# A decoder block's feed-forward start: a second plain pair in the first network, no queued steps behind a unit's last product, and convolution steps handed out earlier

## The chip, the cores and the metric

The kernel runs on one core of one Trainium2 chip. The metric is the device time of one execution in microseconds, the median of several runs. The kernel before takes 1319.47 us (three runs, 1318.66 to 1320.85). The profiled execution took 1317.04 us; its span, from the first to the last instruction, is 1315.2 us.

## The reference

One trunk layer on x of 512 tokens by 1024 channels, all in float32:

```
h = x + 1/2 * SwiGLU_1(rmsnorm(x))            # gate, up: 1024 -> 2816; down: 2816 -> 1024
u = rmsnorm(h)
z = u @ W_in  -> conv GLU (2 x 1024) | q | k | v | merge gates (2 x 1024)
yA = Linear(swish(LayerNorm(causal depthwise conv, 31 taps (GLU))))
yB = Linear(dilated causal window attention, 4 head slots x 3 groups)
h = h + W_o( sigmoid(gA) * yA + sigmoid(gB) * yB )
h = h + 1/2 * SwiGLU_2(rmsnorm(h))
h = h + sigmoid(rmsnorm(h) @ W_pg) * (p @ W_pp)
y = rmsnorm(h)
```

## The kernel before

**Arithmetic.** Every matrix product is float32 made of three passes on TensorE: each operand is split into a high and a low part, and high x high, low x high and high x low are added up in PSUM (`mm3`, L457/458/459, in the 512-wide form). A weight's high part `wh` is an ACT copy, its low part `wl` is either a DVE subtraction (L400 and L401) or is made by a DMA that accumulates: ACT writes the negated copy (L370), GpSimd issues a DMA that adds the weight on top (L372), ACT copies the high part (L384). `by_dma` says which weights go the second way.

**The two networks** run through `ffn(n, ...)`. Gate and up are worked out in 11 pairs of column blocks, each 1024 x 256 of both matrices. A pair comes in one of two forms.

- A *plain* pair (`plain`, called once per half): 96 matmuls of 128x512 on the normal product. It needs the two parts `xsh`, `xsl` of the input and nothing else; the row norm is multiplied onto the result later by `gated` (L815, L816, L818), which frees the pair's PSUM banks.
- A *unit* (`gate_up`): a Strassen-Winograd scheme with seven products B11, B21, T2, T1, T3, B22, T4, 24 matmuls of 128x256 each (`quarters_of`, L732, L733, L735), 168 in all. Products T2 and T1, and T3 and T4, take differences of the input's quarters. `forms` makes them: DVE subtracts (L840), ACT copies the high part `bh` (L827), DVE takes the low part `bl` (L830). The first call makes T1/T2; the function that it returns (`others`) makes T3/T4. The weights' combinations are sums and differences on DVE (`sum_one`, L338, L342, L346, L351). What a product leaves in PSUM is copied by ACT (L931) or added by DVE (L944).

The down products (`down`, L742, L743, L747, added to h by L756/L758) take five of the six rounds of hidden channels in the same seven-product form, with combinations of the hidden activations that `form_pair` makes on DVE and ACT (L663, L675, L678). One round, of the plain pair 0, is plain (`down_plain`, L993 to L1000); its operands `hidh`, `hidl` are made by `keep` (L786, L788).

**What sets the order.** `EARLY` is the number of plain pairs; `PLAN` is the order of units (`gu`) and down products (`dn`, `dp`). Side work waits in two queues of small steps. `jobs` holds `forms` and `gated`; `work(t)` gives out as many of its steps as fit into t us of a product on ACT and DVE. `later` holds `form_pair` and `keep`; `QUOTA` is how many of its steps are issued after each product of a unit. Each step is an instruction in its engine's own program, so what stands before it on that engine also delays it. In front of a product that lacks an operand, the loop `while any(q not in z for z in xn)` issues the queue at once.

**Start of network 1.** Plain pair 0 runs first. In its second half `row_block` transposes x back to rows, eight pieces: TensorE transposes into PSUM (L1096), ACT squares and sums (`Rows.add`, L628) and copies to h (L1098). The row norm's root is `token` (DVE, L632 to L604 and L871), its spread over the partitions `on_all` (two matmuls L609, L610 and an ACT copy L616) gives R. The first unit runs next, and its hooks place `token` behind B11 and, behind B21, R, `gated` and `others`, all drained at once.

**Between the networks.** The convolution is a list `bg` of 240 multiply-adds (L1141) on DVE, with a copy and a running sum for each channel block (`csum`, L1159), given out by `background(n)` beside the products of q, k, v and the merge gates. `N_QK` is how many go beside each q or k unit. Only when `bg` is empty do the gate units give out the LayerNorm's steps `lns`, at most two each: centre (L1497), square, root, L1502, Silu (L1506) and the split `cvh`, `cvl` (L474, L475). What is left of them is issued in a row ahead of the convolution's projection (`py`).

**Network 2** has its `token` and R inside plain pair 0; `gated` and `others` are queued behind it, and `work(10.9)` issues them in one block.

Of the kernel before, what the change touches and what calls it, by code (L numbers as in the profile page):

```python
# [67 lines left out]
EARLY = 1  # L68
# [4 lines left out]
PLAN = (("gu", 1), ("gu", 2), ("gu", 3), ("dn", 1), ("gu", 4), ("gu", 5), ("dn", 2), ("gu", 6), ("gu", 7), ("dn", 3),  # L73
# [6 lines left out]
QUOTA = {"T4": 2, "B11": 3, "B21": 2, "T2": 1, "T1": 3, "T3": 3, "B22": 3}  # L80
# [8 lines left out]
N_QK = ((2, 0, 1),) * 6  # L89
# [29 lines left out]
def ffn_order(n):  # L119
    out = [("gq", n, j, q) for j in range(EARLY) for q in range(4)]  # L120
    for step in PLAN:
        if step[0] == "dp":
            out += [("dp", n, step[1], x_) for x_ in range(2)]
        else:
            out += [(n, step, q) for q in PRODUCTS]
    return out
# [24 lines left out]
def block_kernel(ctx: ExitStack, tc: tile.TileContext, a, out):  # L151
# [101 lines left out]
    def by_dma(key):  # L253
        return (product(key) in BY_DMA or key[0] in POOLED + RAISED or key[:2] == ("gq", "2")
                or key[0] in ("1", "2") and key[1] == ("gu", EARLY))

# [518 lines left out]
    def ffn(n, xs, u, norm, out_, soon_=None, last_=None):  # L775
# [4 lines left out]
        def keep(j, ts, tile_=None):  # L780
            if j >= EARLY:
# [17 lines left out]
        def plain(us_, beside):  # L799

            ps = bank("pg"), bank("pu")
            for k in range(KD):
# [4 lines left out]
                for g, p in ((0, ps[0]), (4, ps[1])):  # L807
                    c = slice((g + k % 4) * P, (g + k % 4 + 1) * P)
                    mm3(p, h[:, c], l[:, c], xs[k][0], xs[k][1], k == 0, k == KD - 1)
            return ps  # L810
# [63 lines left out]
        done = []  # L874
        for half in range(2):
            us_ = [lambda i=i: slab(("gq", n, 0, 2 * half + i)) for i in range(2)]
            fs = {}
            if n == "1" and half:
                fs = {k: turns.pop(0) for k in range(KD)}
            elif n == "2":  # L880
                fs = {k: f for (at, k), f in zip(N_NORM, (token, lambda: R.append(norm.on_all()))) if at == half}
                if half == 0:
                    fs[2] = soon_
            done.append(plain(us_, fs))
            if half == (n == "1"):
                others = forms()
            if n == "2":
                work(10.9)
        hooks = {}
        if n == "1":  # L890
            while jobs:
                next_job()

            def spread(done=done, others=others):
                R.append(norm.on_all("cv"))
                gated(*done)
                while jobs:
                    next_job()
                others()
                done.clear()  # L900
            hooks = {"B11": token, "B21": spread}
        else:
            gated(*done)
# [886 lines left out]
```

## Time and profile before

| what | us |
|---|---|
| median of the runs | 1319.47 |
| the profiled execution | 1317.04 |
| its span | 1315.2 |
| TensorE matmul busy | 1273.8 (97%) |
| VectorE busy | 1054.0 (80%) |
| ScalarE busy | 765.8 (58%) |
| mean granted TensorE clock | 0.989 |

PE is TensorE, PEld its weight loads, DVE VectorE, ACT ScalarE, POOL GpSimd. A row of the timeline has the start in us, the duration, engine, line, operation and out<-in; in brackets stands how long the engine had been idle before, and which instruction ended that. In the waits of an engine stand the waiting instruction, the one that was waited for, the total, how many times, and the longest. PEclk is the granted share of the TensorE clock, 1.00 being full. A matmul's own duration overlaps its neighbours': the pace of TensorE is read from starts.

### The profile page before, as it was taken

What the parts mean: (1) busy time and instruction counts of PE and PEld (TensorE: products, weight loads), DVE (VectorE), ACT (ScalarE), POOL (GpSimd) and SP (SyncE); (2) the same over time, 40 slices, a digit from 0 to 9 for tenths busy, and PEclk for the clock granted to TensorE, in tenths of its full rate; (3) what the DMA queues carried; (4) which work ended last, traced back from release to release, by engine and by line L of the source; (5) the groups of instructions that cost most, each with busy time, mean ns of one, the idle gap of its engine ahead of it and who ended that gap; (6) DMA issues with size and microseconds to landing.
All of it is one profiled execution on the core that took longest, in us unless ns stands there. A gap on an engine that the chain in (4) does not pass through costs nothing. (4 is left out here: it accounts for less than half of the span.)

```text
span 1315.2 us, 20075 instructions
## 1 busy us (share of the span) xinstructions
PE 1273.8 (97%) x7538; PEld 1127.4 (86%) x7538; DVE 1054.0 (80%) x1714; ACT 765.8 (58%) x1116; POOL 238.9 (18%) x308
## 2 busy tenths in 40 slices
PE   8799999999999999999999998999899999999997
PEld 7698989898788889898898886878898989989786
DVE  6579898898779987878886857697689888887975
ACT  8666657566453245646465435365776766665573
POOL 0101111111122232323332221113211111111000
PEclk9899999999999999999999999999999999999999
DMA  7767776866798888988887785659878687776631
GB/s 231 170 164 179 193 192 151 218 156 169 189 208 190 197 174 192 161 175 161 179 166 173 180 202 144 161 134 219 197 188 207 148 207 171 190 200 163 158 96 64
DMA packets 122567, 230.71 MB, mean 175 GB/s; under 512 B 19304, under 2 KB 63720, under 8 KB 122472
## 3 DMA queue, kind: packets, MB, share of 16 engines
q0 software_dynamic: 47872, 144.72, 54.0%
q1 hardware_dynamic: 74312, 84.46, 20.6%
q8 instruction: 59, 0.97, 0.3%
q14 instruction: 36, 0.29, 0.1%
q10 hardware_dynamic: 288, 0.26, 0.1%
HBM read 166.46 MB, written 2.13 MB: 128 GB/s over the span
## 5 line engine op out<-in xcount | busy, mean ns | idle before, releaser
L372 POOL DMA_DIRECT2D wl<-wr x106 | 91.0, 859 | 616.0 <-ACT wl L370 460.2
L1141 DVE SCALAR_TENSOR_TENSOR acc<-glu,taps,acc 128x511 f32<-128x511 f32 (+14 forms) x240 | 161.0, 732 | 0.0
L401 DVE TENSOR_TENSOR wl<-s,wh 128x1024 fp32r<-128x1024 f32 x90 | 109.8, 1220 | 55.0 <-ACT wh L400 55.0
L732 PE MATMUL pa<-bh,wh 128*128 128x256 f32 x480 | 121.3, 289 | 10.5 <-ACT bh L827 6.0
L370 ACT ACTIVATE wl<-wr 128x1024 fp32r<-128x1024 f32 x106 | 111.1, 1048 | 22.9 <-DMA wr<-in_w_ffn_gate 11.2
L733 PE MATMUL pa<-bl,wh 128*128 128x256 f32 x480 | 121.4, 289 | 0.8 <-DVE bl L830 0.7
L370 ACT ACTIVATE wl<-wh 128x1024 fp32r<-128x1024 f32 x80 | 83.7, 1051 | 57.6 <-DMA wh<-in_w_in 29.5
L400 ACT ACTIVATE wh<-s 128x1024 fp32r<-128x1024 f32 x90 | 94.1, 1049 | 35.8 <-DMA wl<-wr 13.1
L384 ACT ACTIVATE wh<-wr 128x1024 fp32r<-128x1024 f32 x106 | 110.8, 1046 | 3.5 <-PE pd L747 1.9
L732 PEld LDWEIGHTS pa<-bh,wh 128*128 128x128 f32 x480 | 94.5, 197 | 11.2 <-ACT bh L827 6.2
L733 PEld LDWEIGHTS pa<-bl,wh 128*128 128x128 f32 x480 | 94.5, 197 | 1.4 <-DVE bl L830 1.3
L372 POOL DMA_DIRECT2D wl<-in_w_in x56 | 48.7, 870 | 222.8 <-ACT wl L370 211.3
L457 PE MATMUL pq<-xsh,wh 128*128 128x512 f32 x224 | 88.7, 396 | 0.0
L458 PE MATMUL pq<-xsl,wh 128*128 128x512 f32 x224 | 87.3, 390 | 0.0
L459 PE MATMUL pq<-xsh,wl 128*128 128x512 f32 x224 | 87.3, 390 | 0.0
L735 PE MATMUL pa<-bh,wl 128*128 128x256 f32 x480 | 69.2, 288 | 0.0
L457 PE MATMUL pg<-xsh,wh 128*128 128x512 f32 x160 | 64.2, 401 | 0.3 <-DVE xsh L485 0.3
L735 PEld LDWEIGHTS pa<-bh,wl 128*128 128x128 f32 x480 | 63.9, 198 | 0.0
L458 PE MATMUL pg<-xsl,wh 128*128 128x512 f32 x160 | 62.9, 393 | 0.8 <-DVE xsl L486 0.6
L459 PE MATMUL pg<-xsh,wl 128*128 128x512 f32 x160 | 62.5, 391 | 0.0
L742 PE MATMUL pa<-wh,bh 128*128 128x512 f32 x136 | 54.6, 401 | 8.1 <-DVE gx L758 8.1
L758 DVE SCALAR_TENSOR_TENSOR gx<-pa,half,gx 128x512 f32<-128x512 f32 x80 | 56.1, 743 | 1.8 <-PE pa L747 1.7
(360 smaller groups left out, 3813.4 us busy)
## 6 DMA issues: line engine op xcount, KB each, us to landing
wl<-wr POOLq DMA_DIRECT2D x106, 512.0 KB, 5.3
wh<-in_w_in POOLq DMA_DIRECT2D x56, 512.0 KB, 7.3
wl<-in_w_in POOLq DMA_DIRECT2D x56, 512.0 KB, 6.1
wr<-in_w_ffn_down SPq DMA_DIRECT2D x44, 512.0 KB, 5.2
wr<-in_w_ffn_up SPq DMA_DIRECT2D x84, 256.0 KB, 4.5
wr<-in_w_ffn_gate SPq DMA_DIRECT2D x82, 256.0 KB, 5.2
wh<-in_w_v POOLq DMA_DIRECT2D x16, 256.0 KB, 7.2
wl<-in_w_v POOLq DMA_DIRECT2D x16, 256.0 KB, 5.8
```

The lines of the kernel that those rows point to most:

```text
L370: A.activation(l.bitcast(F32R), h, AF.Copy, scale=-1.0)
L372: G.dma_start(to, src, accum_op=OP.add)
L384: A.activation(h, r, AF.Copy)
L400: A.activation(h, r, AF.Copy)
L401: V.tensor_sub(l, r, h.bitcast(F32))
L457: PE.matmul(ps, wh, xh, start=start, stop=False, skip_group_check=part)
L458: PE.matmul(ps, wh, xl, start=False, stop=False, skip_group_check=part)
L459: PE.matmul(ps, wl, xh, start=False, stop=stop, skip_group_check=part)
L732: PE.matmul(o, h[:, c], th, start=q in ("B11", "B21", "T1") and i == 0, stop=False, skip_group_check=True)
L733: PE.matmul(o, h[:, c], tl, start=False, stop=False, skip_group_check=True)
L735: PE.matmul(o, l[:, c], th, start=False, stop=i >= len(at) - 2, skip_group_check=True)
L1141: bg.append(lambda acc=acc, g=g, w=w, s=s: V.scalar_tensor_tensor(acc[:, s:], g[:, :S - s], w, acc[:, s:], op0=OP.mult, op1=OP.add))
```

## The change

- `EARLY` becomes 2 for network 1 and stays 1 for network 2, so network 1's pair 1 is plain and its first unit is pair 2. `PLAN` starts at unit 2, with unit 1 ahead of it for network 2 alone. Pair 1's hidden tiles go to `form` like a unit's.
- `QUOTA` gives out nothing behind T4 (before 2), and 4 behind B11 (before 3).
- The first units no longer make all seven of their low parts by accumulating DMA; only B11, B21 and T4 do, as in other units.
- Network 1: `token` stands at the start of pair 1 and R behind its k = 3; behind pair 1's first half `gated` of pair 0 is issued, and `others` is queued into the second half (`plain` now calls `work(1.36)` behind each k). The hooks in the unit are gone.
- Network 2: `gated` is queued behind the plain pair, `others` behind it, and `work(2.9)` instead of `work(10.9)` follows, so that the T3/T4 differences come out with the products of unit 1.
- `row_block` copies from PSUM with DVE, and ACT squares from h.
- Convolution: `background` gives 14 instead of 10 at c == 0, 3 instead of 2 beside the first two of six q/k places in a slot, and four more ahead of each slot's `v0` unit and of the first gate unit.

Line numbers of the changed kernel are one lower than before's up to about L870, five to nine higher behind it.

```diff
--- before.py
+++ after.py
@@ -65,19 +65,19 @@
 A11, A12, A21, A22 = range(4)
 PRODUCTS = ("B11", "B21", "T2", "T1", "T3", "B22", "T4")
 MIXED = ("B11", "T1", "T2", "B22", "T3", "B21", "T4")
-EARLY = 1
+EARLY = {"1": 2, "2": 1}
 
 
 ROUNDS = ((0, 1), (1, 2), (3, 2), (5, 2), (7, 2), (9, 2))
 
-PLAN = (("gu", 1), ("gu", 2), ("gu", 3), ("dn", 1), ("gu", 4), ("gu", 5), ("dn", 2), ("gu", 6), ("gu", 7), ("dn", 3),
+PLAN = (("gu", 2), ("gu", 3), ("dn", 1), ("gu", 4), ("gu", 5), ("dn", 2), ("gu", 6), ("gu", 7), ("dn", 3),
         ("gu", 8), ("gu", 9), ("dn", 4), ("gu", 10), ("dp", 0), ("dn", 5))
 HELD = (3, 5, 7)
 BY_ = False
 N_FORM = 10
 N_LAST = 3
 AFTER_M = {"B11": 2, "T1": 2, "T2": 2, "B22": 2, "T3": 2, "B21": 2, "T4": 2}
-QUOTA = {"T4": 2, "B11": 3, "B21": 2, "T2": 1, "T1": 3, "T3": 3, "B22": 3}
+QUOTA = {"B11": 4, "B21": 2, "T2": 1, "T1": 3, "T3": 3, "B22": 3}
 POOL_MIX = False
 POOL_SUMS = False
 
@@ -86,7 +86,7 @@
 BY_DMA = ("B11", "B21", "T4")
 
 N_GLU = (0, 0) + (6,) * 14
-N_QK = ((2, 0, 1),) * 6
+N_QK = ((3, 0, 1),) * 2 + ((2, 0, 1),) * 4
 N_V0, N_V = 4, 1
 N_TURN = 6
 N_SOON = 2
@@ -117,8 +117,8 @@
 
 
 def ffn_order(n):
-    out = [("gq", n, j, q) for j in range(EARLY) for q in range(4)]
-    for step in PLAN:
+    out = [("gq", n, j, q) for j in range(EARLY[n]) for q in range(4)]
+    for step in (("gu", 1),) * (EARLY[n] == 1) + PLAN:
         if step[0] == "dp":
             out += [("dp", n, step[1], x_) for x_ in range(2)]
         else:
@@ -251,8 +251,7 @@
         return max(c.stop for _, c, _ in srcs)
 
     def by_dma(key):
-        return (product(key) in BY_DMA or key[0] in POOLED + RAISED or key[:2] == ("gq", "2")
-                or key[0] in ("1", "2") and key[1] == ("gu", EARLY))
+        return (product(key) in BY_DMA or key[0] in POOLED + RAISED or key[:2] == ("gq", "2"))
 
     def product(key):
         return key[2] if key[0] in ("1", "2", "m") else None
@@ -778,7 +777,7 @@
         xn = [{} for _ in range(4)]
 
         def keep(j, ts, tile_=None):
-            if j >= EARLY:
+            if j:
                 waiting.append((j, ts, tile_))
                 return
             hl = [(T("hidh", F32R), T("hidl", F32R)) for _ in ts]
@@ -807,6 +806,7 @@
                 for g, p in ((0, ps[0]), (4, ps[1])):
                     c = slice((g + k % 4) * P, (g + k % 4 + 1) * P)
                     mm3(p, h[:, c], l[:, c], xs[k][0], xs[k][1], k == 0, k == KD - 1)
+                work(1.36)
             return ps
 
         def gated(pgs, pus):
@@ -871,39 +871,46 @@
             V.tensor_scalar(t, y, 0.5, None, op0=OP.mult)
             half_r.append(t)
 
-        done = []
-        for half in range(2):
-            us_ = [lambda i=i: slab(("gq", n, 0, 2 * half + i)) for i in range(2)]
-            fs = {}
-            if n == "1" and half:
-                fs = {k: turns.pop(0) for k in range(KD)}
-            elif n == "2":
-                fs = {k: f for (at, k), f in zip(N_NORM, (token, lambda: R.append(norm.on_all()))) if at == half}
-                if half == 0:
-                    fs[2] = soon_
-            done.append(plain(us_, fs))
-            if half == (n == "1"):
-                others = forms()
-            if n == "2":
-                work(10.9)
-        hooks = {}
+        def factor():
+            R.append(norm.on_all("cv" if n == "1" else "ps"))
+
+        for j in range(EARLY[n]):
+            done = []
+            for half in range(2):
+                us_ = [lambda i=i: slab(("gq", n, j, 2 * half + i)) for i in range(2)]
+                fs = {}
+                if n == "2":
+                    fs = {k: f for (at, k), f in zip(N_NORM, (token, factor)) if at == half}
+                    if half == 0:
+                        fs[2] = soon_
+                elif (j, half) == (0, 1):
+                    others = forms()
+                    fs = {k: turns.pop(0) for k in range(KD)}
+                elif (j, half) == (1, 0):
+                    fs = {0: token, 4: factor}
+                done.append(plain(us_, fs))
+                if (j, half) == (1, 0):
+                    rest = jobs[:]
+                    jobs.clear()
+                    gated(*before)
+                    while jobs:
+                        next_job()
+                    jobs.extend(rest)
+                    before = None
+                    others()
+                if n == "2" and half == 0:
+                    others = forms()
+            before = done
+        rest = jobs[:]
+        jobs.clear()
+        gated(*before)
         if n == "1":
-            while jobs:
-                next_job()
-
-            def spread(done=done, others=others):
-                R.append(norm.on_all("cv"))
-                gated(*done)
-                while jobs:
-                    next_job()
-                others()
-                done.clear()
-            hooks = {"B11": token, "B21": spread}
+            jobs.extend(rest)
+            job(lambda: (keep(1, early[1], early[1]), form()))
         else:
-            gated(*done)
             others()
-            work(10.9)
-        done = others = None
+        work(2.9)
+        done = others = before = None
 
         def both_halves(half):
             return bass.AP(tensor=R[0].tensor, offset=R[0].offset + half.start, ap=[R[0].ap[0], [0, 2], [1, 256]])
@@ -924,8 +931,6 @@
                 while any(q not in z for z in xn):
                     next_job()
                 quarters_of(p, q, wh, wl, [z[q] for z in xn])
-                if q in hooks:
-                    hooks.pop(q)()
                 if q in ("B11", "T2", "T1"):
                     t[q] = T("p")
                     A.activation(t[q], p, AF.Copy)
@@ -1004,7 +1009,7 @@
                     work(2 * k_ * 0.68)
             hid.clear()
 
-        for key in PLAN:
+        for key in (("gu", 1),) * (EARLY[n] == 1) + PLAN:
             if key[0] == "gu":
                 if key[1] == KF // 2 - 2:
                     keep(0, early[0])
@@ -1094,8 +1099,9 @@
         p = bank("tp", "cv")
         for i in range(KD // 2):
             PE.transpose(p[:, i * P:(i + 1) * P], by_class(x[4 * j + i])[:, b], ident)
-        norm.add(b, j, p)
-        A.activation(h[b][:, j * S:(j + 1) * S], p, AF.Copy)
+        V.tensor_copy(h[b][:, j * S:(j + 1) * S], p)
+        norm.add(b, j)
+        spend(0.69, 0.74)
 
     def over(xs, v, ks, us_=None):
 
@@ -1195,7 +1201,7 @@
             unit(z[2], ("win", c), us)
             glu(*z, (1,))
         if c == 0:
-            background(10)
+            background(14)
             rc, rs = tabs["cos"], tabs["sin"]
             for t in (rc, rs):
                 bg.append(lambda t=t: V.tensor_mul(t, t, R[0]))
@@ -1430,6 +1436,7 @@
         q, k = [], []
         now = Attention(q, k)
         p = bank("pq")
+        background(N_V0)
         unit(p, ("v0", s), us, beside=before.last() if before else {})
         v0 = T("v0")
         V.tensor_mul(blocks(v0), by_block(p), by_block(R))
@@ -1543,6 +1550,8 @@
     for base in (48, 40):
         for m in range(KD):
             p = bank("pg")
+            if not n:
+                background(N_V0)
             unit(p, ("win", base + m), us, beside={4: half} if n else before.last())
             t = T("sg")
             V.tensor_mul(t, p, R)
```

DVE at the start of network 1, before: the norm's R exists, and `gated` (tg, tu), the weight sums of the next unit (s) and the T3/T4 differences (t_560 on, with bl) follow.

```order
L818 TENSOR_TENSOR tu_552<-pg_272,tg_550 128x512
L818 TENSOR_TENSOR tu_553<-pu_273,tg_551 128x512
L944 TENSOR_TENSOR p_505<-p_505,pe_520 128x512
L338 TENSOR_TENSOR s_135_599<-wr_440,wr_443 128x1024
L342 TENSOR_TENSOR s_140_633<-s_135_599,wr_446 128x1024
L840 TENSOR_TENSOR t_560<-u_170,u_134 128x256
L840 TENSOR_TENSOR t_560<-u_170,t_399 128x256
L840 TENSOR_TENSOR t_563<-u_185,u_144 128x256
L840 TENSOR_TENSOR t_563<-u_185,t_400 128x256
L840 TENSOR_TENSOR t_566<-u_191,u_154 128x256
L840 TENSOR_TENSOR t_566<-u_191,t_401 128x256
L830 TENSOR_TENSOR bl_562<-t_560,bh_561 128x512
```

The same place of DVE in the changed kernel. Here pg_203 and pu_204 are the banks of plain pair 0's first half, pg_278 and pu_279 those of its second; there are six such banks, and pair 1's first half takes the other two.

```order
L421 TENSOR_TENSOR wl_495<-wr_239,wh_494 128x1024
L337 TENSOR_TENSOR s_107_498<-wr_292,wr_295 128x1024
L815 TENSOR_TENSOR tg_529<-pg_203,R_492 128x512
L815 TENSOR_TENSOR tg_530<-pu_204,R_492 128x512
L818 TENSOR_TENSOR tu_531<-pg_278,tg_529 128x512
L818 TENSOR_TENSOR tu_532<-pu_279,tg_530 128x512
L341 TENSOR_TENSOR s_128_553<-s_107_498,wr_298 128x1024
L840 TENSOR_TENSOR t_539<-u_170,u_134 128x256
L840 TENSOR_TENSOR t_539<-u_170,t_266 128x256
L840 TENSOR_TENSOR t_542<-u_180,u_144 128x256
L345 TENSOR_TENSOR wr_292<-wr_298,wr_292 128x1024
L840 TENSOR_TENSOR t_542<-u_180,t_267 128x256
```

The differences stand behind one weight sum more (s_107 ahead of tg, s_128 behind tu), and all of it is now beside a plain pair.

DVE at the merge gates and the convolution's projection, before; `sg<-pg` is a gate unit (the last of them is row sg_7770, 34 rows above this piece), `sg<-sg,pb` the attention's projection, and cv the channel blocks of the convolution.

```order
L1571 TENSOR_TENSOR sg_7310<-sg_7310,pb_7920 128x512
L1571 TENSOR_TENSOR sg_7353<-sg_7353,pb_7939 128x512
L1571 TENSOR_TENSOR sg_7407<-sg_7407,pb_7953 128x512
L1502 TENSOR_TENSOR cv_4728<-cv_4728,R_7967 128x512
L1502 TENSOR_TENSOR cv_4775<-cv_4775,R_7967 128x512
L1502 TENSOR_TENSOR cv_5920<-cv_5920,R_7967 128x512
L1502 TENSOR_TENSOR cv_5922<-cv_5922,R_7967 128x512
L1502 TENSOR_TENSOR cv_7105<-cv_7105,R_7967 128x512
L1502 TENSOR_TENSOR cv_7140<-cv_7140,R_7967 128x512
L475 TENSOR_TENSOR cvl_7978<-cv_4728,cvh_7977 128x512
L475 TENSOR_TENSOR cvl_7983<-cv_4775,cvh_7982 128x512
```

The same steps in the changed kernel, where sg_7761 is the last of the 16 gate units.

```order
L1557 TENSOR_TENSOR sg_7631<-pg_7563,R_4052 128x512
L1557 TENSOR_TENSOR sg_7664<-pg_7634,R_4052 128x512
L1509 TENSOR_TENSOR cv_4588<-cv_4588,R_7667 128x512
L1509 TENSOR_TENSOR cv_4597<-cv_4597,R_7667 128x512
L1509 TENSOR_TENSOR cv_5569<-cv_5569,R_7667 128x512
L1509 TENSOR_TENSOR cv_5576<-cv_5576,R_7667 128x512
L1557 TENSOR_TENSOR sg_7704<-pg_7670,R_4052 128x512
L1509 TENSOR_TENSOR cv_6524<-cv_6524,R_7667 128x512
L1509 TENSOR_TENSOR cv_6572<-cv_6572,R_7667 128x512
L474 TENSOR_TENSOR cvl_7711<-cv_4588,cvh_7710 128x512
L474 TENSOR_TENSOR cvl_7716<-cv_4597,cvh_7715 128x512
```

The steps from R on have moved from behind the attention's projection to among the last three gate units. The last pair of channel sums (csum) has moved from behind the 13th gate unit to behind the seventh.

DVE in network 2's first unit, before: the differences of T3/T4 stand in one block, behind `gated` (tu).

```order
L818 TENSOR_TENSOR tu_8974<-pg_8904,tg_8972 128x512
L818 TENSOR_TENSOR tu_8975<-pu_8905,tg_8973 128x512
L840 TENSOR_TENSOR t_8976<-u_8759,u_8686 128x256
L840 TENSOR_TENSOR t_8976<-u_8759,t_8876 128x256
L840 TENSOR_TENSOR t_8979<-u_8770,u_8697 128x256
L840 TENSOR_TENSOR t_8979<-u_8770,t_8877 128x256
L840 TENSOR_TENSOR t_8982<-u_8781,u_8714 128x256
L840 TENSOR_TENSOR t_8982<-u_8781,t_8878 128x256
L830 TENSOR_TENSOR bl_8978<-t_8976,bh_8977 128x512
L840 TENSOR_TENSOR t_8985<-u_8792,u_8725 128x256
L840 TENSOR_TENSOR t_8985<-u_8792,t_8879 128x256
```

In the changed kernel they stand among the unit's weight splits (wl) and weight sums (s):

```order
L840 TENSOR_TENSOR t_8869<-u_8657,t_8774 128x256
L400 TENSOR_TENSOR wl_8971<-wr_8537,wh_8970 128x1024
L840 TENSOR_TENSOR t_8872<-u_8668,u_8595 128x256
L840 TENSOR_TENSOR t_8872<-u_8668,t_8775 128x256
L400 TENSOR_TENSOR wl_9004<-s_1434_8892,wh_9003 128x1024
L337 TENSOR_TENSOR s_1451_9007<-wr_8894,wr_8897 128x1024
L840 TENSOR_TENSOR t_8875<-u_8679,u_8612 128x256
L341 TENSOR_TENSOR s_1456_9043<-s_1451_9007,wr_8900 128x1024
L840 TENSOR_TENSOR t_8875<-u_8679,t_8776 128x256
L830 TENSOR_TENSOR bl_8871<-t_8869,bh_8870 128x512
L840 TENSOR_TENSOR t_8878<-u_8690,u_8623 128x256
L840 TENSOR_TENSOR t_8878<-u_8690,t_8777 128x256
```

The first bl now stands behind wl_9004, the low part of B22's weight, and the sums s_9007 and s_9043 of the next unit.

## The prediction

> **What bounds the kernel now.** I read the page first, for the busy shares:
>
> ```profile
> PE 1273.8 (97%) x7538; PEld 1127.4 (86%) x7538; DVE 1054.0 (80%) x1714; ACT 765.8 (58%) x1116; POOL 238.9 (18%) x308
> ```
>
> TensorE is busy 97% of the span, 1273.8 us, so the most that reordering can win without touching its work is the other 3%, some 40 us, and what the granted clock costs. The waits of PE say who owns that idle time (columns: total us, times, longest):
>
> ```profile
> PE pa L742 <- DVE gx L758: 8.1, 4, 2.1
> PE pa L732 <- ACT bh L827: 6.0, 1, 6.0
> PE pa L732 <- ACT p L931: 4.3, 1, 4.3
> PE R L609 <- DVE diag L604: 2.6, 1, 2.6
> PE py L457 <- ACT cvh L474: 2.4, 1, 2.4
> PE py L458 <- DVE cvl L475: 2.2, 4, 1.6
> PE tp L1096 <- ACT gx L1098: 1.5, 2, 0.8
> ```
>
> They are few and long, and lie in four places: the first unit of network 1 (bh, diag), the first of network 2 (p), the opening of a down product after the last gate/up (gx), and the conv projection (cvh, cvl). The windows on these places give the clock (columns: length, then busy time of PE, PEld, DVE, ACT, POOL, PEclk, DMA share, GB/s):
>
> ```profile
> 40.00:72.00 32.00, 22.36 (x140) 21.02 (x139) 19.98 (x49) 16.22 (x22) 5.03 (x6) 0.79 0.73 172
> 290.00:310.00 20.00, 18.04 (x86) 14.37 (x86) 17.39 (x22) 12.70 (x15) 3.40 (x4) 1.00 0.78 194
> 380.00:810.00 430.00, 429.57 (x2244) 368.52 (x2242) 341.37 (x652) 211.13 (x354) 119.92 (x160) 1.00 0.85 180
> 800.00:820.00 20.00, 15.83 (x63) 12.01 (x63) 14.42 (x39) 11.67 (x16) 1.44 (x3) 0.91 0.64 164
> 920.00:940.00 20.00, 15.70 (x96) 14.42 (x95) 15.74 (x28) 17.02 (x22) 4.95 (x6) 0.93 0.80 183
> 1170.00:1190.00 20.00, 18.04 (x80) 14.64 (x79) 16.65 (x21) 11.87 (x15) 2.65 (x4) 0.91 0.71 178
> ```
>
> A clock of 0.79 over 32 us is 6.7 us of work lost; 0.91 over 20 us is 1.8. So a wait is followed by a stretch of half clock that costs nearly as much again. Between 380 and 810 us PE waits for nothing (429.57 of 430) and DVE is at 79%: there nothing can be won, only lost.
>
> **First network, start.** The unit lengths come from first matmuls of neighbours in the timeline: a plain pair runs 512-wide matmuls, six of them from 924.69 to 926.05; the first unit starts at 35.90, the second at 71.86, the third at 92.02.
>
> ```profile
> 924.69 0.39 PE L457 MATMUL pg<-xsh,wh 128*128 128x512 f32 x1
> ...
> 926.05 0.28 PE L732 MATMUL pa<-xsh,wh 128*128 128x256 f32 x1
> ```
> ```profile
> 35.90 0.28 PE L732 MATMUL pa<-xsh,wh 128*128 128x256 f32 x1
> ...
> 71.86 0.28 PE L732 MATMUL pa<-xsh,wh 128*128 128x256 f32 x1
> ...
> 92.02 0.28 PE L732 MATMUL pa<-xsh,wh 128*128 128x256 f32 x1
> ```
>
> A plain pair is 96 matmuls at 1.36/6 = 0.227 us, 21.8 us; an undisturbed unit is 92.02 - 71.86 = 20.2 us; the first one takes 36.0, because its own chain cannot keep up:
>
> ```profile
> 40.77 0.16 DVE L632 SCALAR_TENSOR_TENSOR m<-rows 128x4 f32<-128x4 f32 x1
> ...
> 45.00 0.16 DVE L871 TENSOR_SCALAR half<-y 128x4 f32<-128x4 f32 x1
> ...
> 48.91 0.69 DVE L815 TENSOR_TENSOR tg<-pg,R 128x512 f32<-128x512 f32 x1 [3.75 <-ACT R L616]
> ...
> 56.31 1.22 DVE L342 TENSOR_TENSOR s<-s,wr 128x1024 f32<-128x1024 f32 x1 [3.00 <-DMA wl<-wr]
> 57.45 0.42 DVE L840 TENSOR_TENSOR t<-u,u 128x256 f32<-128x256 f32 x1
> ```
>
> The norm factor takes 45.0 - 40.8 = 4.2 us on DVE, R comes back at 48.9, and the T3/T4 differences (L840) come next on DVE behind the weight sum L342, which waits 3.00 us for a DMA until 56.3. The change puts a plain pair there, which needs neither R nor differences. The same chain then runs beside the pair: the eight PSUM copies go to DVE at 0.69 each (the L815 row, also a 128x512 read of PSUM), which takes away the transposes' wait of 1.5, so pair 0 ends at about 35.9 - 1.5 = 34.4. The norm chain starts there and ends near 38.6; R's matmuls stand behind k = 4 of pair 1, by PE's count at 34.4 + 24 x 0.227 = 39.9, so they need not wait. They are two of 512 columns, 2 x 0.227 = 0.45 us. Behind the norm chain DVE has two weight splits and L337 (1.22 each, as L342), four bl (0.69, the size of L815), two differences (0.42) and the two L815 that empty pair 0's banks: 8.6 us, so they end at 38.6 + 8.6 = 47.2, or 46.3 as a step starts some 0.08 before the last one ends (57.45 against 56.31 + 1.22). PE wants the bank at 34.4 + 0.45 + 48 x 0.227 = 45.8. I take a wait of 0.9 there, between none and 1.8. Pair 1 ends at 34.4 + 21.8 + 0.45 + 0.9 = 57.6, against 71.9 now: **-14.3**. Bounds: -15.2 if nothing waits, about -8 under the first rival. In unit 2, which is now the first to need T3, the differences are queued in pair 1's second half, some 11 us (48 x 0.227) before the unit starts and 22 before its fifth product; I see no wait.
>
> [...]
>
> **Opening of the down product after the fourth group.** T4, a unit's last product, no longer hands out two queued steps (2 of the quota; B11 takes one more). In the trace DVE waits for ACT's weight copy wh, and PE for DVE:
>
> ```profile
> 297.53 1.23 DVE L401 TENSOR_TENSOR wl<-s,wh 128x1024 fp32r<-128x1024 f32 x1 [1.96 <-ACT wh L400]
> ...
> 299.56 0.47 PE L742 MATMUL pa<-wh,bh 128*128 128x512 f32 x1 [1.96 <-DVE gx L758]
> ```
>
> The same happens at this place in network 2, where the steps ahead of wh on ACT, L675's b and (not shown) bh, can be seen waiting for the sum u:
>
> ```profile
> 1175.21 0.42 ACT L675 ACTIVATE b<-u 128x256 fp32r<-128x256 f32 x1 [3.10 <-DVE u L936]
> ...
> 1179.17 0.61 PE L742 MATMUL pa<-wh,bh 128*128 128x512 f32 x1 [1.96 <-DVE gx L758]
> ```
>
> Without these steps wh is done before DVE gets to it, and both waits of 1.96 go: -2.0 in network 1, and in network 2 -2.0 and the half clock behind it, 1.8 by the 1170 window: **-5.8**. Bounds: -3 if wh is held by the DMA instead, -6. The two other L742 waits (2.1 each, behind the plain down product) are left alone: what DVE does there has the same sum.
>
> **Conv and its norm.** 31 multiply-adds of the conv (two pairs of N_QK groups, four ahead of each slot's v0, four ahead of the first gate unit, four at c == 0) run earlier.
>
> ```profile
> L1141 DVE SCALAR_TENSOR_TENSOR acc<-glu,taps,acc 128x511 f32<-128x511 f32 (+14 forms) x240 | 161.0, 732 | 0.0
> ```
>
> At 0.73 each at most that is 23 us of DVE work taken off the far end. The last channel sums come behind the 13th of the 16 gate units now, behind the 7th in the changed order, and all eight L1502 steps stand ahead of the sum of the last gate unit, not in front of the projection. So py's waits, 2.4 + 2.2, go, and the half clock (0.91 in the 800 window, 1.8): **-6.4**; -3 if one of the waits stays with its half clock. The cost lies in cover: DVE rises from 341 to 364 of the 430 us at most, if none of these steps had been in them; PE has no wait there and I cost it at nothing, up to +5 if four slots wait 1.2 each, the length of one weight sum. Two more table loads on ACT cost nothing, since ACT is at 211 of 430.
>
> **Second network, first unit.** Only T3/T4 are moved: before, they were drained while PE waited.
>
> ```profile
> 935.64 0.57 ACT L931 ACTIVATE p<-pa 128x512 f32<-128x512 f32 x1
> ...
> 946.48 0.28 PE L732 MATMUL pd<-xsh,wh 128*128 128x256 f32 x1
> ```
>
> ACT came to p only at 935.64, PE waited 4.3, and T3 ended where the sixth product starts, at 946.5. Now p comes right behind B11, so T2 need not wait: that alone is -4.3, and -1.4 of half clock (0.93 over 20 us), together -5.7. At 20.2 / 7 = 2.9 us a product, T2 ends at 934.7 and T3 could start at 937.6. But T3 wants bl, and in the changed order DVE reaches the first bl behind the weight split of B22, which waits for ACT, and ACT stands behind T2's copy: 934.7 + 0.57 for the copy + 0.6 for a bh + about 1.1 for the weight (twice the columns) = 937.0. Then follow on DVE that split, two weight sums (1.22 each) and two differences (0.42): 4.5, so bl starts at 941.5; with four bl and two differences more, 3.6, the last one ends at 945.1. Half of T3's last quarter is left then, so it ends between 946 and 948: a new wait takes the place of the old one, **+0.7**, between -5.7 (no wait) and +3 (a half clock behind it).
>
> **Sum, on the profiled execution (1317.04 us):** -14.3 - 5.8 - 6.4 + 0.7 = **-25.8**, 1291.2. The median of the runs is 1319.47, 2.43 above that execution; so **1293.7**.
>
> **Rivals.** (1) *A weight sum holds pair 1.* L337, a sum of two weight tiles for unit 2, stands ahead of the L815 steps on DVE; if its tiles are late, as at 56.31 (3.00 us), pair 0's banks are kept, PE waits up to 5 us in the middle of pair 1 and half clock costs 1.8: the start is worth 14.3 - (5 + 1.8 - 0.9) = 8.4, and the time is 1293.7 + 5.9 = 1299.6. For: the DMA was at 0.73 over 40 to 72, and two plain pairs read weights just as fast. Against: the 7 accumulating transfers of the first unit go. (2) *The conv's gain stays out:* DVE late in the slots, or the projection waits as before: +6.4 and up to 5, 1300.1 to 1305.1. For: DVE is the busiest engine after PE. Against: it has 89 us free in those 430, and no PE wait. (3) *No new wait at T3:* DVE reaches the differences in time; 1293.7 - 6.4 = 1287.3. For: DVE was busy 15.7 of 20 us at 920 to 940 with the whole block drained at once. Against: the order puts B22's split ahead of bl. (4) *The half clocks are not of these waits.* At 299.56 a wait of 1.96 stands as at 1179.17, and only the latter has lost clock beside it (1.00 in 290 to 310, 0.91 in 1170 to 1190). If the 1.8 at 800 and the 1.8 at 1170 stay, the time is 1293.7 + 3.6 = 1297.3. [...] (5) *Slower:* the steps T4 no longer takes pile up and come due at the down products. There are ten; the gain of 5.8 there goes, and from (25.8 - 5.8) / 10 = 2.0 us each the change loses: at 4.3 us each, what the drained steps cost T2 in network 2, it is 1293.7 + 5.8 + 43 = 1342.5. For: L742 already heads the waits. Against: the quota falls only from 17 to 16 a unit.
>
> **How the numbers follow.** Forecast 0.50 (its own range 1290 to 1298: nothing waits in pair 1 and the first network gains 0.9 more with 2 to 3 less at T3, or T3 costs 2 more and the down products give 2 less); rival 1 0.17, 2 0.14, 3 0.06, 4 0.09, 5 0.04. The range 1287 to 1304 holds all these but 5, the upper end of 2, and 1 and 2 together, under 0.2 in all. A measurement of this kernel tells 0.2% (2.6 us) from no change. Every case but 5 is faster by more; what is left for no change is a sum of several mishaps: 0.94 faster, 0.02 same, 0.04 slower.
>
> **What would show it.** Right: second unit's first matmul near 57.6 with clock 1.00 in 40 to 72; no wait of PE for R or bh there; the openings after the fourth group without the 1.96; py without a wait; a wait of 4 to 5.5 us in T3 of network 2, on bl. Wrong: a wait on tg in pair 1 over 2 us, PE waits between 380 and 810, or a longer list of L742 waits.

## The result, and the profile after

The changed kernel takes 1284.38 us (four runs, 1284.28 to 1289.34) against 1319.07 of before (1318.08 to 1320.85): a ratio of 0.9745, interval 0.9719 to 0.977. The forecast was 1293.7, its range 1287.0 to 1304.0: the direction was right, the gain larger than the range allowed, 34.7 us for 25.8. The profiled execution is the longest of the four, 1289.34 (span 1287.2, mean clock 0.995); the three others took 1284.28 to 1284.48 at 0.996 and 0.997. So the trace shows 27.7 us of gain, close to the forecast only because the profiled execution is 5.0 us over its kernel's median; the rest is in executions that it does not show.

What PE waits for now:

```profile
PE pa L741 <- DVE gx L757: 4.2, 2, 2.6
PE pa L732 <- DVE bl L830: 4.0, 1, 4.0
PE warm L503 <- DVE one L497: 1.1, 1, 1.1
PE pg L456 <- DVE tg L815: 0.9, 1, 0.9
PE pb L456 <- ACT xsh L476: 0.8, 1, 0.8
```

R, bh, p, cvh, cvl and tp are gone from the list. The wait on gx (DVE adds a down product's result to h, which frees the PSUM bank that PE wants next) is down from 8.1 in four to 4.2 in two. The 0.9 on tg, in the middle of network 1's pair 1, and the 4.0 on bl, in network 2's T3, are the two new waits that were forecast. The same five stages in windows:

```profile
40.00:58.00 18.00, 17.08 (x78) 13.92 (x77) 16.17 (x28) 11.80 (x16) 1.84 (x2) 1.00 0.49 118
361.00:771.00 410.00, 410.00 (x2160) 352.67 (x2159) 341.33 (x652) 210.42 (x356) 113.93 (x152) 1.00 0.83 177
780.00:800.00 20.00, 20.00 (x90) 16.54 (x90) 7.68 (x13) 6.57 (x8) 7.07 (x10) 1.00 0.96 232
900.00:925.00 25.00, 20.99 (x150) 20.49 (x150) 17.94 (x27) 14.30 (x19) 2.57 (x3) 0.86 0.47 109
1195.00:1215.00 20.00, 17.37 (x70) 13.84 (x69) 18.11 (x26) 10.05 (x13) 0.86 (x1) 0.91 0.70 188
```

The start of network 1 has lost no clock (1.00, before 0.79). PE has no wait between 361 and 771, nor at the convolution's projection (780 to 800). Lost clock has moved to T3 (0.86 over 25 us, 3.5 us) and to the last down product of network 2 (0.91 over 20, 1.8).

Read from first matmuls in the two timelines, with the forecast's terms:

| stage | forecast | by the traces |
|---|---|---|
| start of network 1, to the start of unit 2 | -14.3 | 71.86 to 57.41: -14.4 |
| the two openings after the fourth group | -5.8 | -2.2 and -3.4: -5.5 |
| other down products, both networks | 0 | -0.7, -0.9 (the third of each); -1.5 and +1.1 from the plain product on |
| from q/k/v to network 2's first unit | -6.4 | -7.7 |
| network 2's first units, to its first down product | +0.7 | +1.7 |

What is left of 28.0 us of span lies in steps of 0.5 us or less.

T3 of network 2, DVE first and then PE:

```profile
910.40 1.23 DVE L400 TENSOR_TENSOR wl<-s,wh 128x1024 fp32r<-128x1024 f32 x1 [1.54 <-ACT wh L399]
911.55 1.22 DVE L337 TENSOR_TENSOR s<-wr,wr 128x1024 f32<-128x1024 f32 x1
...
913.02 1.22 DVE L341 TENSOR_TENSOR s<-s,wr 128x1024 f32<-128x1024 f32 x1
...
914.49 0.68 DVE L830 TENSOR_TENSOR bl<-t,bh 128x512 fp32r<-128x512 f32 x1
```
```profile
915.23 0.58 PE L732 MATMUL pa<-bl,wh 128*128 128x256 f32 x1 [3.96 <-DVE bl L830]
```

The split wl of B22 waits for ACT, two weight sums follow, and bl starts at 914.49. The whole program lies 26.6 us earlier here (899.48 for 926.05), so the forecast's 941.5 is 914.9 on this axis.

### The profile page after: what moved, and what is told of

It is laid out like the page before. It is cut to its first block, busy times and chain, and to the rows that moved or that the text cites. A ratio compares the mean times of both kernels' runs of the same rounds, so it can differ in the third digit from the quotient of the medians.

```text
span 1287.2 us, 19870 instructions
## 1 busy us (share of the span) xinstructions
PE 1265.8 (98%) x7466; PEld 1122.6 (87%) x7466; DVE 1062.2 (83%) x1724; ACT 750.6 (58%) x1093; POOL 229.5 (18%) x297
## 5 line engine op out<-in xcount | busy, mean ns | idle before, releaser
L369 ACT ACTIVATE wl<-wr 128x1024 fp32r<-128x1024 f32 x101 | 106.1, 1050 | 19.9 <-DVE wl L400 5.7
L732 PE MATMUL pa<-bl,wh 128*128 128x256 f32 x456 | 113.6, 286 | 4.0 <-DVE bl L830 4.0
L731 PE MATMUL pa<-bh,wh 128*128 128x256 f32 x456 | 113.2, 285 | 0.3 <-DVE p L949 0.3
L383 ACT ACTIVATE wh<-wr 128x1024 fp32r<-128x1024 f32 x101 | 105.8, 1047 | 8.4 <-PE pd L746 6.2
L732 PEld LDWEIGHTS pa<-bl,wh 128*128 128x128 f32 x456 | 88.6, 194 | 4.5 <-DVE bl L830 4.5
L731 PEld LDWEIGHTS pa<-bh,wh 128*128 128x128 f32 x456 | 88.5, 194 | 0.5 <-DVE p L949 0.5
L456 PE MATMUL pg<-xsh,wh 128*128 128x512 f32 x176 | 70.9, 403 | 1.1 <-DVE tg L815 0.9
L457 PE MATMUL pg<-xsl,wh 128*128 128x512 f32 x176 | 69.4, 394 | 0.7 <-DVE xsl L485 0.4
L458 PE MATMUL pg<-xsh,wl 128*128 128x512 f32 x176 | 68.7, 390 | 0.0
L936 ACT ACTIVATE p<-pa 128x512 f32<-128x512 f32 x38 | 22.7, 598 | 69.4 <-PE pa L734 69.0
```

What stands on the lines that cost most here:

```text
L369: A.activation(l.bitcast(F32R), h, AF.Copy, scale=-1.0)
L383: A.activation(h, r, AF.Copy)
L456: PE.matmul(ps, wh, xh, start=start, stop=False, skip_group_check=part)
L457: PE.matmul(ps, wh, xl, start=False, stop=False, skip_group_check=part)
L458: PE.matmul(ps, wl, xh, start=False, stop=stop, skip_group_check=part)
L731: PE.matmul(o, h[:, c], th, start=q in ("B11", "B21", "T1") and i == 0, stop=False, skip_group_check=True)
```

## The experiments

**The same kernel again, and three single edits.** They ran on one chip with 14 runs of before: median 1317.92, 1312.14 to 1323.62.

> The changed kernel itself once more. Its profiled execution took 1289.3 us, three others 1284.3 to 1284.5. Theory A (half clock by chance): the waits are the same in all executions, and the 5.1 us are the half-clock stretches behind the T3 wait of network 2 (6.83 us long, 3.4 lost) and behind the last down product's wait (3.41 long, 1.7 lost), which most executions do not get: median 1284 to 1285, and a profile of a short execution shows PE idle as before within 0.5 us and one or both stretches gone. Theory B (shorter waits): a short execution has the T3 wait under 2 us or the transfers' waits gone, with the same half clock.

1286.93 (1285.48 to 1288.31), ratio 0.9774, interval 0.9753 to 0.9795: 31.0 us of gain here. Its profiled execution took 1286.55. The wait at T3 is the same to 0.01, and so is its half clock; behind the last down product the wait was 1.5 instead of 2.6, with no clock lost:

```profile
910.00:925.00 15.00, 10.99 (x72) 10.50 (x72) 9.79 (x15) 7.27 (x10) 1.71 (x2) 0.77 0.38 71
1198.00:1210.00 12.00, 10.49 (x46) 8.21 (x45) 12.00 (x16) 7.97 (x11) 0.86 (x1) 1.00 0.67 171
```

1.1 of wait and 1.8 of clock make the 2.8 us between the two profiled executions. So neither theory holds whole: behind the down product both the wait and the half clock were shorter, and the long wait at T3 is in both executions with its half clock. No execution of 1284 was profiled; that they lack part of the half clock at T3 is only suggested, by mean clocks of 0.996 and 0.997 for 0.995.

The convolution's places alone:

```diff
-N_QK = ((2, 0, 1),) * 6
+N_QK = ((3, 0, 1),) * 2 + ((2, 0, 1),) * 4
...
-            background(10)
+            background(14)
...
+        background(N_V0)
...
+            if not n:
+                background(N_V0)
```

> The kernel before with only the convolution's steps handed out earlier. Forecast's term: -6.4 us, 1312.7. Read from the two traces between the start of the q/k/v stage and network 2 it is -7.7, 1311.4. Rival (DVE in the slots pays for it): no gain, or waits of PE between 380 and 770 us of over 3 us in all.

1309.94, ratio 0.9945 (0.9927 to 0.9964), 8.0 us by the medians. First the kernel before in the stage of the attention slots, then this kernel at the projection and in the slots:

```profile
380.00:770.00 390.00, 390.00 (x2065) 336.23 (x2064) 321.24 (x604) 196.52 (x336) 110.00 (x146) 1.00 0.84 178
```
```profile
795.00:815.00 20.00, 20.00 (x90) 16.59 (x89) 7.73 (x12) 10.28 (x13) 5.66 (x8) 1.00 0.75 182
380.00:770.00 390.00, 390.00 (x2071) 336.31 (x2070) 330.82 (x624) 200.93 (x344) 110.42 (x147) 1.00 0.84 179
```

DVE does 9.6 us more in the slots at no cost to PE, and the projection runs without a wait. The rival is out. In the timelines the gain from q/k/v to network 2 is 8.3, more than the 6.4 of waits and clock. Part of that may be that a wait costs more than its listed length: two matmuls of before, at 811.98 and 814.07, start 2.1 us apart where 0.23 is the usual pace, so 1.9 is lost at a listed wait of 1.6. What the rest is was not traced.

The quota alone:

```diff
-QUOTA = {"T4": 2, "B11": 3, "B21": 2, ...
+QUOTA = {"B11": 4, "B21": 2, ...
```

> The kernel before with only the quota changed: nothing behind T4, four behind B11. Forecast's term: -5.8 us, 1313.3, both waits of 1.96 gone. From the traces of after: -2.2 and -3.4 at the two openings and 0.4 to 0.9 at each of two or three other down products, -6 to -7.5 in all, 1311.6 to 1313. Rival (steps pile up at the down products): slower, a longer list of waits of the down products.

1306.50, ratio 0.992 (0.9901 to 0.9938): 11.4 us by the medians, twice the forecast's term.

```profile
PE py L458 <- DVE cvl L475: 1.8, 2, 1.6
PE pa L742 <- DVE gx L758: 1.7, 2, 0.9
PE pd L997 <- DMA wl<-wr: 1.6, 2, 0.9
```

Gx is down from 8.1 in four to 1.7 in two: not only the two waits of 1.96 are gone, those behind the plain down product are 0.9 each for 2.1. The steps do not pile up, so the prediction's rival 5 is out too. By the timelines the two openings gave 2.2 and 3.3, as forecast; the third down product of each network 0.7 and 0.9, and the stretch of plain and last down product 2.5 and 1.2. The forecast had put these last four at nothing.

Why the waits behind the plain product fall is to be seen on DVE 15 us and more before them, where it adds up weight tiles for the last down product. In network 1, before:

```profile
330.89 1.22 DVE L338 TENSOR_TENSOR s<-wr,wr 128x1024 f32<-128x1024 f32 x1 [1.21 <-DMA wr<-in_w_ffn_down]
...
338.71 1.23 DVE L342 TENSOR_TENSOR s<-s,wr 128x1024 f32<-128x1024 f32 x1 [5.27 <-DMA wr<-in_w_ffn_down]
```

With only the quota changed:

```profile
328.50 1.23 DVE L338 TENSOR_TENSOR s<-wr,wr 128x1024 f32<-128x1024 f32 x1 [0.37 <-DMA wr<-in_w_ffn_down]
...
330.97 1.22 DVE L342 TENSOR_TENSOR s<-s,wr 128x1024 f32<-128x1024 f32 x1
```

In network 2 these waits are 1.53 and 3.91 before, and none with the quota alone. So DVE had stood idle for a load, and all its work behind that came later.

The rest of the change alone: the changed kernel with the two diffs above undone.

> The changed kernel with the quota and the convolution's places as before: what is left is the second plain pair, the PSUM copies on DVE, fewer accumulating transfers in the first units and the spread differences in network 2. Forecast: -14.3 + 0.7 = -13.6, 1305.5; by the trace of after -14.5 + 1.7 = -12.8, 1306.3, and by the short executions 3.4 less, 1303. Rival (terms not additive): under 10 us, over 1309.

1303.09, ratio 0.9897 (0.9878 to 0.9915): 14.8 us by the medians, 13.6 by the ratio of 1317.92. The terms add within the noise: 13.6 + 7.2 + 10.5 = 31.3 by the three ratios, against 29.8 for the whole change by its own.

**The spread differences of network 2.** These four ran on another chip, before 1317.55 (11 runs, 1311.75 to 1319.14).

```diff
-        work(2.9)
+        work(10.9)
```

> The changed kernel with all of network 2's queued differences issued behind the plain pair at once, as before the change. Theory (the wait only moved): T3's wait of 3.96 on bl goes, T2's wait of about 4.3 on p comes back, with about as much half clock: within 2 us of the changed kernel, 1284 to 1288. Rival (spreading was worth the forecast's -5.7): 5 us slower, 1290 to 1292.

1279.45 (1278.21 to 1281.94), ratio 0.9716 (0.9697 to 0.9735). Neither theory said this: issued in one block (the *drained* kernel from here on), the differences cost less than spread, and the kernel beats the changed one, whose eight runs in two other sets took 1284.28 to 1289.34. The traces say the same of this stage alone: from the first matmul of network 2's first unit to that of its first down product it takes 62.4 us, in the changed kernel 68.2 and 67.6. The old wait did not come back whole:

```profile
PE pa L741 <- DVE gx L757: 2.6, 2, 1.6
PE pa L731 <- ACT p L936: 1.7, 1, 1.7
```
```profile
898.00:925.00 27.00, 25.33 (x209) 25.05 (x209) 24.17 (x35) 18.57 (x26) 2.57 (x3) 1.00 0.61 157
```

T2 waits 1.7 on p, not 4.3, without lost clock. On ACT only one weight copy stands between the last bh and p:

```profile
903.74 0.63 ACT L827 ACTIVATE bh<-t 128x512 fp32r<-128x512 f32 x1 [0.58 <-DVE t L840]
904.28 1.04 ACT L399 ACTIVATE wh<-s 128x1024 fp32r<-128x1024 f32 x1
905.23 0.58 ACT L936 ACTIVATE p<-pa 128x512 f32<-128x512 f32 x1
```

Half of the differences ahead of the unit:

```diff
-        work(2.9)
+        work(5.8)
```

> The changed kernel with 5.8 instead of 2.9 us of queued steps issued ahead of network 2's first unit, so that about half of the T3/T4 differences stand ahead of the weight splits. Theory (T3 waits for what stands ahead of bl on DVE, T2 for what stands ahead of p on ACT): T3's wait falls by 1 to 2 us and T2 does not wait over 1: 1 to 3 us below the changed kernel. Rival: T2 waits as much as T3 gains, no change.

1283.94 (1283.08 to 1287.88). The wait at T3 did not fall: 4.5 in the profiled execution, 1287.88.

```profile
911.53 1.23 DVE L400 TENSOR_TENSOR wl<-s,wh 128x1024 fp32r<-128x1024 f32 x1 [1.05 <-ACT wh L399]
912.67 1.22 DVE L337 TENSOR_TENSOR s<-wr,wr 128x1024 f32<-128x1024 f32 x1
913.92 1.22 DVE L341 TENSOR_TENSOR s<-s,wr 128x1024 f32<-128x1024 f32 x1
915.07 1.29 DVE L830 TENSOR_TENSOR bl<-t,bh 128x512 fp32r<-128x512 f32 x2
```

The last two bl still stand behind B22's split and both sums. What matters is the last bl, not how many are early. The theory was right on the cause and wrong on the remedy; the rival, that T2 takes over the wait, is not seen either.

Two plain pairs in network 2 as well:

```diff
-EARLY = {"1": 2, "2": 1}
+EARLY = {"1": 2, "2": 2}
...
```

The lines left out keep the norm's steps and the first call of `forms` in network 2's pair 0.

> The changed kernel with two plain pairs in network 2 also. The differences then run beside a plain pair: T3's wait of 3.96 and the half clock behind it (3.4) go, a plain pair costs 1.6 more than a unit: -5.8 us, about 1280 where the changed kernel takes 1286. Rival (the wait moves into the pair, as 0.9 on tg in network 1, or the queue is late for the next unit): -2 or less.

1280.17 (1279.84 to 1280.89), ratio 0.972 (0.9703 to 0.9738). Waits and clock of that stage are gone, as expected:

```profile
898.00:945.00 47.00, 47.00 (x305) 43.14 (x304) 30.11 (x44) 24.59 (x36) 6.10 (x7) 1.00 0.63 145
```

It is level with the drained kernel: a plain pair takes 1.6 us more than a unit, about the 1.7 that the drained kernel waits at T2.

T4's steps dropped, B11 left at three, in the kernel before:

```diff
-QUOTA = {"T4": 2, "B11": 3, "B21": 2, ...
+QUOTA = {"B11": 3, "B21": 2, ...
```

> The kernel before with only T4's two queued steps dropped from the quota and nothing added to B11. Theory (the steps behind T4 stand ahead of what the down product's opening needs): as the whole quota edit, 9 to 11 us below before, with both waits of 1.96 gone and the wait behind the plain down product near 0.9 in place of 2.1. Rival (the steps of B11 matter, or the queue now runs over into the down products): under 6.

1310.32, ratio 0.9948 (0.9933 to 0.9963): 7.2 us, between theory and rival. The openings are clear, but the waits behind the plain product have grown to 2.9:

```profile
PE pa L742 <- DVE gx L758: 5.9, 2, 2.9
```

So T4's part gives about 7 us (6.9 by its ratio), and B11's fourth step the rest of the quota's 10.5, some 3.7 us. The two ran on different chips and their intervals touch, but the waits on gx, 2.9 each here for 0.9 each, show the step's effect in the traces.

**What holds p, where the copies are, and a fifth step.** On a third chip, before 1318.3 (9 runs, 1313.69 to 1321.3). First the drained kernel with the accumulated low parts again:

```diff
-        return (... or key[:2] == ("gq", "2"))
+        return (... or key[:2] == ("gq", "2")
+                or key[:2] == ("2", ("gu", 1)))
```

> The kernel with network 2's differences drained at once (1279.5 us), with all seven low parts of network 2's first unit made by accumulating DMA again, as in the kernel before. Theory (ACT's two extra passes per accumulated low part stand ahead of p, more than the drained differences do): T2's wait of 1.67 grows to about 4.3, with half clock behind it, 1283 to 1286. Rival (the drained differences alone hold p): the wait stays near 1.7, 1279 to 1280.

1284.61 (1282.86 to 1285.63): 5.2 us over the drained kernel by the medians, 3.2 by the ratios on the two chips, and 4.2 in the traces of this stage (66.6 us for 62.4). The wait on p is 4.6, and ACT shows why:

```profile
902.83 0.63 ACT L828 ACTIVATE bh<-t 128x512 fp32r<-128x512 f32 x1 [0.64 <-DVE t L841]
903.37 1.04 ACT L370 ACTIVATE wl<-s 128x1024 fp32r<-128x1024 f32 x1
904.31 1.04 ACT L384 ACTIVATE wh<-s 128x1024 fp32r<-128x1024 f32 x1
905.26 1.04 ACT L370 ACTIVATE wl<-wr 128x1024 fp32r<-128x1024 f32 x1
906.21 1.04 ACT L384 ACTIVATE wh<-wr 128x1024 fp32r<-128x1024 f32 x1
907.15 0.57 ACT L937 ACTIVATE p<-pa 128x512 f32<-128x512 f32 x1
```

Four weight passes stand between the last bh and p where the drained kernel has one. They are in the kernel before too:

```profile
931.32 0.63 ACT L827 ACTIVATE bh<-t 128x512 fp32r<-128x512 f32 x1 [0.64 <-DVE t L840]
931.85 1.04 ACT L370 ACTIVATE wl<-s 128x1024 fp32r<-128x1024 f32 x1
932.80 1.04 ACT L384 ACTIVATE wh<-s 128x1024 fp32r<-128x1024 f32 x1
933.75 1.04 ACT L370 ACTIVATE wl<-wr 128x1024 fp32r<-128x1024 f32 x1
934.69 1.04 ACT L384 ACTIVATE wh<-wr 128x1024 fp32r<-128x1024 f32 x1
```

The theory holds, though an accumulated low part costs ACT one pass more than a subtracted one (L370), not two: of before's wait at T2, the larger part was the accumulated low parts, which the change takes away as well.

The changed kernel with ACT's copies again:

```diff
-        V.tensor_copy(h[b][:, j * S:(j + 1) * S], p)
-        norm.add(b, j)
+        norm.add(b, j, p)
+        A.activation(h[b][:, j * S:(j + 1) * S], p, AF.Copy)
```

> The changed kernel with the eight PSUM copies of the first plain pair on ACT again, which squares from PSUM. Forecast's working: the transposes wait 1.5 again, and pair 1 inherits it, +1.5 us. Rival (the norm chain on DVE is due earlier when DVE has no copies, and the wait of 0.9 on tg goes): +0.6 or less, no difference to be told.

1285.64 (1284.7 to 1287.44), ratio 0.9751: no difference from the changed kernel's 0.9745 and 0.9774. The transposes wait again, and the wait on tg is gone.

```profile
PE tp L1101 <- ACT gx L1103: 0.9, 1, 0.9
```

The rival holds: whichever engine copies, DVE reaches tg at the same time (45.5 us here, 45.6 in the changed kernel).

The drained kernel, and the one with two plain pairs in both networks, with a fifth step:

```diff
-QUOTA = {"B11": 4, ...
+QUOTA = {"B11": 5, ...
```

> The kernel with network 2's differences drained at once (1279.5 us), with five queued steps behind B11 instead of four. Theory (the fourth step behind B11 is what cut the wait behind the plain down product from 2.9 to 0.9 by bringing the queue forward; a fifth does the same again): these two waits, 1.0 and 1.6 there, fall by 0.5 to 1 each, 1277.5 to 1279. Rival (the fifth step stands ahead of what a product needs): waits at B21 or T2 of the units, 1280 or more.

> The kernel with two plain pairs in both networks (1280.2 us), with five queued steps behind B11. Same theory: the two waits behind the plain down products, 1.2 and 0.9 there, fall by 0.5 to 1 each, 1278.5 to 1279.5; same rival, 1281 or more.

1285.77 (1283.12 to 1286.1) and 1284.05 (1281.67 to 1285.24), by the medians 6.3 and 3.9 us worse than the kernels without the step. By the ratios on the two chips that is 4.0 and 2.0, with intervals that overlap. In the traces the stretches from the plain down products on are 5.8 and 6.4 us longer in all, part of it half clock. The theory falls, and the waits at B21 or T2 that the rival named are not there either (T2 waits 1.1 on p, in the drained kernel 1.7). The waits behind the plain product are 2.9. The drained kernel with the fifth step, its waits and its weight sum on DVE:

```profile
PE pa L741 <- DVE gx L757: 5.8, 2, 2.9
```
```profile
315.58 1.23 DVE L337 TENSOR_TENSOR s<-wr,wr 128x1024 f32<-128x1024 f32 x1 [4.16 <-DMA wr<-in_w_ffn_down]
...
320.11 1.22 DVE L341 TENSOR_TENSOR s<-s,wr 128x1024 f32<-128x1024 f32 x1 [1.98 <-DMA wr<-in_w_ffn_down]
```

The drained kernel without it:

```profile
312.91 1.22 DVE L337 TENSOR_TENSOR s<-wr,wr 128x1024 f32<-128x1024 f32 x1
...
315.37 1.22 DVE L341 TENSOR_TENSOR s<-s,wr 128x1024 f32<-128x1024 f32 x1
```

DVE waits 4.16 and 1.98 for the last down product's weights, does the sum 4.7 us later, and everything behind it slips. The loads' issue on SP goes with it: in all eight profiles with four steps behind B11 and none behind T4, the third of the six loads of this stage is issued 11.4 us after the first, in both networks; in all six with another quota, 12.7 to 13.7 us after it. The queue's own waits tell what that load waits for, in the changed kernel and in the kernel before:

```profile
SPq L268 <- DVE wl L400: 4.4, 1, 4.4
```
```profile
SPq L269 <- DMA wl<-wr: 5.9, 1, 5.9
```

In all eight it waits 4.4 us for a low part that DVE subtracts, in all six others 5.8 to 6.6 us for an accumulating transfer. So the quota changes which instruction frees the third load's buffer. Why it does was not tried and stays open, and the early issue is not the whole of it: in network 2 of the changed kernel's first profile DVE still waits 3.83 us for these weights, and PE 2.6 behind the plain product.

## Why the prediction was wrong

- **Start of network 1: right.** -14.3 forecast, -14.4 in the traces, with the forecast wait of 0.9 on tg. One part of its working was idle: the PSUM copies on DVE win nothing, since the transposes' wait and the wait on tg stand for each other. That the sum fits so closely is therefore partly luck. L337 was not late; rival 1 did not happen.
- **Openings after the fourth group: right**, -5.8 forecast and -5.5 in the traces; dropping T4's steps alone clears both.
- **The failing step: "The two other L742 waits (2.1 each, behind the plain down product) are left alone: what DVE does there has the same sum."** The sum of DVE's work is the same, but not when it can start: in before's trace DVE stands idle 5.27 us at 338.71 for the weights of the last down product, a wait that the prediction did not price, and the quota changes when those weights are loaded. With the quota alone the two waits of PE there fell from 2.1 to 0.9, worth 2.5 and 1.2 us in the timelines where the forecast had nothing. The third down products, also at nothing, gave 0.7 and 0.9; PE had no wait over 0.2 us there, and what they gained from is not shown. In all the quota was worth 10.5 us by its ratio (11.4 by the medians), with an interval of 8.2 to 13.0, not 5.8.
- **Convolution: right within the noise.** 6.4 forecast, 7.2 by the ratio (4.7 to 9.6), and 7.7 and 8.3 in the traces, so perhaps a little small: waits were priced at their listed length. PE paid nothing in the slots; rival 2 did not happen.
- **Network 2: the new wait right, the cause of the gain wrong.** The wait on bl came where it was put, 4.0 us, and +1.7 for +0.7 is inside its bounds; rival 3 did not happen. But the forecast credited T2's gain to the moved differences ("Only T3/T4 are moved"). It came mostly from the accumulated low parts: with those gone and the differences drained as before, the kernel is 1279.45. The spreading itself costs 5 to 6 us here by the traces.
- **The range** had no room left for this. By the ratios the other terms together were off by about a microsecond, the quota by 5. In the second set of runs the gain was 31.0 us, which gives 1288.5 on the forecast's basis, just inside; with the first set's 34.7 it is outside. What sets the two sets apart is not shown.
- **Rival 4**, that half clock is not of these waits, was too simple: it comes with waits, but not with each of them nor in each execution, as the last section shows. So the half clock in the forecast's terms (1.8 at the opening in network 2, 1.8 at the convolution) was that of one execution.

## What to carry to other kernels

Where a wait follows a backlog, ask what started the backlog: the same work on an engine can be due earlier when the load that it waits for is issued earlier, and a table that only sets the order of small steps can move that load (here the third of six was issued 11.4 us after the first, with other quotas 12.7 to 13.7, and DVE's wait of 5.27 us in network 1 was gone with the quota alone). Two edits that act on one wait have to be undone one at a time: here the gain at T2 belonged mostly to the DMA edit, and the reordering beside it cost some 5 us. When a block of work is spread out, look at its last piece, since the product waited for the last operand and not for the mean: with half of the differences issued early, T3 still waited 4.5 us for the last bl, for 4.0 in the changed kernel.

## What the runs showed of the hardware

Whether a wait of some 2 us is followed by half clock differs between equal waits. Of two waits of 1.96 us, before lost clock at network 2's (0.91 in 1170 to 1190) and not at network 1's (1.00 in 290 to 310); in the kernel with only the convolution's change it is the other way round:

```profile
290.00:310.00 20.00, 18.04 (x78) 14.49 (x78) 17.28 (x22) 11.71 (x15) 2.46 (x4) 0.91 0.69 177
1165.00:1185.00 20.00, 18.04 (x78) 13.98 (x78) 17.89 (x22) 11.83 (x14) 2.57 (x3) 1.00 0.79 195
```

A lost stretch costs about 1.7 us, or twice that, as at T3's wait of 4.0: in the clock records of the traces it is 3.41 us at half clock, or a multiple of that. Up to the end of PE's work, before has four stretches of 3.41 us and one of 10.24, which begins within the wait of 6.0 on bh; the changed kernel has one of 6.83 at T3's wait and one of 3.41 behind the wait of 2.6 on gx. Over the fourteen traces, no single wait of PE of 1.7 us or less was followed by one, two of six of 1.96 were, three of six of 2.1, and eleven of twelve of 2.6 to 3.0. What decides between equal waits no run shows.
